# Batch normalisation streamed through one DMA ring: parameters as sixteen equal rows between the halves of the first tile

## The chip, the cores and the metric

The kernel runs on one core of a Trainium2 chip. The metric is the device time of one execution in microseconds (us).

Some words used throughout. The **ring** is the queue of transfers that one issuing engine (here SyncE) hands to the core's 16 DMA engines; it is first in, first out on each of them. A **packet** is one piece of a transfer on one DMA engine; here a packet is a 64 KB row of a tile. A **turn** is the place on the ring where a load is followed by a store. The **spread** of a transfer is the time between the first and the last of its 16 semaphore packets, that is, between the DMA engine that finishes it first and the one that finishes it last. "Packet records" are the trace's list of single packets (start, duration, size), from which I read what the printed views average away; a slow packet is a 64 KB packet that took over 32 ns longer than the usual 2418 ns. Packet times are counted from the start of the span.

## The reference, cut to what matters

```python
# x: [32, 256, 128, 128] float32; gamma, beta, running_mean, running_var: [256]
return gamma * (x - mean) / np.sqrt(var + 1e-5) + beta      # per channel
```

One multiply and one add per element: 537 MB are read and 537 MB written.

## The kernel before

A tile is 128 channels by 128x128 pixels: 128 rows of 64 KB, 8.39 MB, 64 tiles. There are three tile buffers, of 64 KB per channel row. All tile loads and stores go through SyncE's ring; the four parameter vectors go through ScalarE's.

```python
rows = params.tile([B, C], f32, tag="rows")                  # B = 32, C = 256
nc.vector.memset(rows, 0.0)
for r, ap in enumerate((running_var, gamma, beta, running_mean)):
    nc.scalar.dma_start(out=rows[r : r + 1, :], in_=ap.rearrange("(o c) -> o c", o=1))
for i in range(NBUF):                                        # NBUF = 3
    load(i)                                                  # nc.sync.dma_start(out=t[:], in_=xr[i])
...
nc.vector.transpose(out=turned[:], in_=rows[:])              # rows to columns, in 32x32 blocks
... # four copies, square root on ScalarE, reciprocal, two multiplies, a subtraction
for i in range(NT):                                          # NT = 64
    compute(i)                                               # tensor_scalar: t * scale + shift, in place
    store(i)                                                 # nc.sync.dma_start(out=outr[i], in_=t[:])
    if 1 <= i and i + 2 < NT:
        load(i + 2)                                          # into the buffer that store i-1 frees
```

## Time and profile before

| | before |
|---|---|
| time, median of 3 runs | 2486.44 us (2485.47 to 2487.72) |
| span of the profiled run | 2486.6 us |
| DMA bytes and mean rate | 1073.77 MB, 432 GB/s |
| VectorE busy | 566.0 us, 23% |
| first compute starts | 24.78 us |
| spread of the last store | 7.78 us (packet records) |

The prediction below shows the lines behind this table and how they are read.

### The profile page before, as it was taken

To read this page: it belongs to the slowest core of one execution; us is meant where nothing else is said; L and a number is where in the kernel's file an instruction comes from. 1 tells how busy PE (TensorE), PEld (TensorE's weight loads), DVE (VectorE), ACT (ScalarE), POOL (GpSimd) and SP (SyncE) were. 2 spreads that over 40 slices of the span, in tenths; PEclk is the share of its full clock that TensorE was granted. 3 is DMA by queue.
4 is the path that set the end of the run, shared out by engine and by line. 5 is a ranking of instruction groups with operands and counts; after the bars stand their busy time and mean duration, and the time that the engine had idled before them with its cause. 6 is when DMAs were issued, how large, how long until landed. Compare 5 with 4: busy or idle time off the path is not lost.

```text
span 2486.6 us, 384 instructions
## 1 busy us (share of the span) xinstructions
DVE 566.0 (23%) x75; ACT 1.6 (0%) x2; POOL 0.2 (0%) x4
## 2 busy tenths in 40 slices
DVE  3122121221212212122121221222212212122121
ACT  0000000000000000000000000000000000000000
POOL 0000000000000000000000000000000000000000
DMA  9999999999999999999999999999999999999998
GB/s 421 423 439 433 431 431 435 435 425 436 433 435 426 438 436 430 432 438 434 433 432 435 434 433 433 436 434 430 436 436 432 430 439 434 433 431 436 434 434 380
DMA packets 18442, 1073.77 MB, mean 432 GB/s; under 512 B 2052, under 2 KB 2056, under 8 KB 2056
## 3 DMA queue, kind: packets, MB, share of 16 engines
q1 hardware_dynamic: 18432, 1073.75, 99.8%
q14 instruction: 2, 0.02, 0.0%
q10 hardware_dynamic: 8, 0.00, 0.0%
HBM read 536.88 MB, written 536.87 MB: 432 GB/s over the span
## 4 chain that ended last, share of the span: by engine, by line
another core or an unknown queue 72%; DVE 22%; DMA 4%; issue 0%; DVEq 0%; ACTq 0%; ACT 0%; SPq 0%
DVE t L89 22%; DMA out_dram<-t 2%; DMA t<-in_x_dram 2%; DMA rows<-in_running_mean_dram 1%; DVEq L89 0%; ACTq L54 0%; DVE par L67 0%; DVE turned L62 0%; ACT tmp_t L74 0%; DVE rows L52 0%; DVE tmp_t L81 0%; DVE shift_t L84 0%; DVE tmp_t L83 0%; DVE scale_t L82 0%
## 5 line engine op out<-in xcount | busy, mean ns | idle before, releaser
L89 DVE TENSOR_SCALAR t<-t,scale_t,shift_t 128x16384 f32<-128x16384 f32 x64 | 564.0, 8812 | 1867.1 <-DMA t<-in_x_dram 1867.0
L62 DVE STREAM_TRANSPOSE turned<-rows 32x256 f32<-32x256 f32 x1 | 0.4, 433 | 21.4 <-DMA rows<-in_running_mean_dram 21.4
L74 ACT ACT_TABLE_LOAD x1 | 1.3, 1283 | 2.6 <-issue 2.6
L67 DVE COPY par<-turned 32x8 f32<-32x8 f32 x4 | 0.6, 162 | 0.1
L52 DVE MEMSET rows<- 32x256 f32 x1 | 0.3, 272 | 0.8 <-PEq L122 0.8
L74 ACT ACTIVATE tmp_t<-par,eps_t 128x2 f32<-128x2 f32 x1 | 0.3, 296 | 19.8 <-DVE par L67 19.8
L81 DVE RECIPROCAL tmp_t<-tmp_t 128x2 f32<-128x2 f32 x1 | 0.2, 165 | 0.4 <-ACT tmp_t L74 0.4
L83 DVE TENSOR_TENSOR tmp_t<-par,scale_t 128x2 f32<-128x2 f32 x1 | 0.2, 161 | 0.0
L84 DVE TENSOR_TENSOR shift_t<-par,tmp_t 128x2 f32<-128x2 f32 x1 | 0.2, 161 | 0.0
L82 DVE TENSOR_TENSOR scale_t<-par,tmp_t 128x2 f32<-128x2 f32 x1 | 0.2, 160 | 0.0
L122 POOL MEMSET const-bfloat16-1.0<- 128x1 bf16 x1 | 0.1, 102 | 0.0
L122 POOL MEMSET const-uint8-127<- 128x1 uint8 x1 | 0.1, 101 | 0.0
L122 POOL MEMSET const-float32-0.0<- 128x1 f32 x1 | 0.1, 98 | 0.2 <-issue 0.2
L122 POOL MEMSET const-float32-1.0<- 128x1 f32 x1 | 0.1, 98 | 0.0
L60 DVE MEMSET eps_t<- 128x1 f32 x1 | 0.1, 59 | 0.0
## 6 DMA issues: line engine op xcount, KB each, us to landing
t<-in_x_dram SPq DMA_DIRECT2D x64, 57.9
out_dram<-t SPq DMA_DIRECT2D x64, 49.0
rows<-in_running_var_dram ACTq DMA_DIRECT2D x1, 1.0 KB
rows<-in_gamma_dram ACTq DMA_DIRECT2D x1, 1.0 KB
rows<-in_beta_dram ACTq DMA_DIRECT2D x1, 1.0 KB
rows<-in_running_mean_dram ACTq DMA_DIRECT2D x1, 1.0 KB
```

What stands on the lines that cost most here:

```text
L52: nc.vector.memset(rows, 0.0)
L60: nc.vector.memset(eps_t, eps)
L62: nc.vector.transpose(out=turned[:], in_=rows[:])
L67: nc.vector.tensor_copy(out=par[q * B : (q + 1) * B], in_=blocks[:, :, q, 0:4])
L74: nc.scalar.activation(out=tmp_t[:], in_=var_t, func=mybir.ActivationFunctionType.Sqrt, bias=eps_t[:], scale=1.0,)
L81: nc.vector.reciprocal(out=tmp_t[:], in_=tmp_t[:])
L82: nc.vector.tensor_mul(out=scale_t[:], in0=gamma_t, in1=tmp_t[:])
L83: nc.vector.tensor_mul(out=tmp_t[:], in0=mean_t, in1=scale_t[:])
L84: nc.vector.tensor_sub(out=shift_t[:], in0=beta_t, in1=tmp_t[:])
L89: nc.vector.tensor_scalar(out=t[:], in0=t[:], scalar1=scale_t[:, cb : cb + 1], scalar2=shift_t[:, cb : cb + 1], op0=mybir.AluOpType.mult, ...
L122: nc = _bacc.Bacc("TRN2", target_bir_lowering=False, num_devices=1)
```

## The change

The intent: bring the parameters in early and on the same ring, so that the first tile can be computed as soon as it lands, and give every DMA engine the same share of them, so that none falls behind the others. Each parameter is read into sixteen equal rows (one per DMA engine) side by side in one wide tile; the transpose then yields sixteen equal columns, of which one is used.

```diff
-    rows = params.tile([B, C], f32, tag="rows")
-    nc.vector.memset(rows, 0.0)
+    t = data.tile([P, HW], f32, tag="t")
+    tiles[0] = t
+    nc.sync.dma_start(out=t[:, left], in_=xr[0][:, left])
+    rows = params.tile([B, NPAR * C], f32, tag="rows")      # NPAR = 4
+    nc.vector.memset(rows[:], 0.0)
     for r, ap in enumerate((running_var, gamma, beta, running_mean)):
-        nc.scalar.dma_start(out=rows[r : r + 1, :], in_=ap.rearrange("(o c) -> o c", o=1))
-    for i in range(NBUF):
-        load(i)
+        nc.sync.dma_start(out=rows[0:NE, r * C : (r + 1) * C], in_=ap.partition_broadcast(NE))  # NE = 16
+    nc.sync.dma_start(out=t[:, right], in_=xr[0][:, right])
+    load(1)
+    load(2)
 ...
-    turned = params.tile([B, C], f32, tag="turned")
+    turned = params.tile([B, NPAR * C], f32, tag="turned")
 ... # (cut: the four copies pick column 0 of each block; same number of instructions)
```

The main loop is the same in both.

More of the change, by code (lines that the diff above doesn't have):

```diff
@@ L34 @@
     NQ = P // B
+    NE = 16
+    NPAR = 4
     params = ctx.enter_context(tc.tile_pool(name="params", bufs=1))
@@ L43 @@
     tiles = {}
+    left, right = slice(0, HW // 2), slice(HW // 2, HW)
     def load(i):
@@ L48, in load @@
         tiles[i] = t
-    rows = params.tile([B, C], f32, tag="rows")
-    nc.vector.memset(rows, 0.0)
+    t = data.tile([P, HW], f32, tag="t")
[3 more added lines that the diff above has]
+    nc.vector.memset(rows[:], 0.0)
     for r, ap in enumerate((running_var, gamma, beta, running_mean)):
-        nc.scalar.dma_start(out=rows[r : r + 1, :], in_=ap.rearrange("(o c) -> o c", o=1))
-    for i in range(NBUF):
-        load(i)
+        nc.sync.dma_start(out=rows[0:NE, r * C : (r + 1) * C], in_=ap.partition_broadcast(NE))
+    nc.sync.dma_start(out=t[:, right], in_=xr[0][:, right])
+    load(1)
+    load(2)
     eps_t = params.tile([P, 1], f32, tag="eps")
-    nc.vector.memset(eps_t, eps)
-    turned = params.tile([B, C], f32, tag="turned")
+    nc.vector.memset(eps_t[:], eps)
+    turned = params.tile([B, NPAR * C], f32, tag="turned")
     nc.vector.transpose(out=turned[:], in_=rows[:])
-    par = params.tile([P, NCB, 4], f32, tag="par")
-    blocks = turned.rearrange("p (cb q r) -> p cb q r", cb=NCB, q=NQ)
+    par = params.tile([P, NPAR, NCB], f32, tag="par")
+    blocks = turned.rearrange("p (rc q b) -> p rc q b", q=NQ, b=B)
+    flat = par.rearrange("p r cb -> p (r cb)")
     for q in range(NQ):
-        nc.vector.tensor_copy(out=par[q * B : (q + 1) * B], in_=blocks[:, :, q, 0:4])
-    var_t, gamma_t, beta_t, mean_t = (par[:, :, r] for r in range(4))
+        nc.vector.tensor_copy(out=flat[q * B : (q + 1) * B], in_=blocks[:, :, q, 0])
+    var_t, gamma_t, beta_t, mean_t = (par[:, r] for r in range(NPAR))
     scale_t = params.tile([P, NCB], f32, tag="scale")
```

## The prediction

> **What bounds the kernel now.** I read the page first: engine totals, the forty slices, the queues.
>
> ```profile
> DVE 566.0 (23%) x75; ACT 1.6 (0%) x2; POOL 0.2 (0%) x4
> ...
> DMA  9999999999999999999999999999999999999998
> ...
> q1 hardware_dynamic: 18432, 1073.75, 99.8%
> q14 instruction: 2, 0.02, 0.0%
> q10 hardware_dynamic: 8, 0.00, 0.0%
> HBM read 536.88 MB, written 536.87 MB: 432 GB/s over the span
> ```
>
> VectorE, the only busy compute engine, works 23% of the span; the DMA engines are busy in every slice. Queue q1 holds everything that SyncE issues: 64 loads and 64 stores of 8.39 MB. Its 18432 packets are 128 x 144, so a transfer is 128 rows of 64 KB (8 on each of 16 DMA engines) and 16 semaphore packets. Queue q10 is the four parameter loads from ScalarE's ring: four rows of 1 KB, four semaphores.
>
> Next the waits of SyncE's queue, to see whether the ring ever runs dry.
>
> ```profile
> SPq L100 <- DVE t L89: 1765.2, 63, 38.2
> SPq L47 <- DMA out_dram<-t: 640.3, 61, 30.8
> ```
>
> A cycle is 28.0 us in which a store waits for its compute (1765.2 / 63) and 10.5 us in which the next load waits for the store before it (640.3 / 61), together 38.5 us. These are the issuer's waits, not the DMA engines'. When store i is issued, store i-1 has 10.5 us to run, and a load of 19.3 us is queued behind it. The ring thus holds about 30 us of work at its lowest.
>
> Then the head, in the timeline.
>
> ```profile
> 2.21 0.36 ACTq L54 DMA_DIRECT2D rows<-in_running_mean_dram  x1
> 2.60 1.28 ACT L74 ACT_TABLE_LOAD   x1 [2.60 <-issue]
> 22.48 0.43 DVE L62 STREAM_TRANSPOSE turned<-rows 32x256 f32<-32x256 f32 x1 [21.36 <-DMA rows<-in_running_mean_dram]
> 22.95 0.69 DVE L67 COPY par<-turned 32x8 f32<-32x8 f32 x4
> ...
> 24.78 8.81 DVE L89 TENSOR_SCALAR t<-t,scale_t,shift_t 128x16384 f32<-128x16384 f32 x1
> 33.63 17.47 SPq L100 DMA_DIRECT2D out_dram<-t  x2
> ```
>
> The parameters take 20 us to land; the first tile is computed at 24.78 us and its store is issued at 33.63 us. That looks like a late start, but the ring at 33.63 us still holds loads 1 and 2, which end near 61 us (the DMA packet records have the semaphores of the third load at 60.6 us).
>
> Last the tail, in windows:
>
> ```profile
> 2470.00:2480.00 10.00, 0.00 (x0) 0.00 (x0) 0.00 (x0) 1.00 0.85 367
> 2480.00:2487.00 7.00, 0.00 (x0) 0.00 (x0) 0.00 (x0) 1.00 0.13 56
> ```
>
> The columns that count are the last two, DMA share and GB/s. The engines do not finish together. The packet records say how far apart: of the last store's 16 semaphores the first is at 2477.32 us, the last at 2485.10, a spread of 7.78 us. For the first load it is 0.45 us, for transfer 20 it is 3.4, for 44 it is 7.8, and it stays at 7.7 to 7.8 from there on.
>
> So the time is a sum, all from packet records: 1.73 us to the first packet; 128 transfers at the fastest engine's pitch of 19.319 us, 2472.8 us; 2.8 us of early slow packets that even that engine has; together 2477.3. Then 7.8 us of spread, and 1.5 us from the last semaphore to the end of the span: 2486.6.
>
> **What the Trainium skill says.** All four places are in "DMA: Bandwidth & Descriptors". (1) Its section "Queues, rings and completion order": each DMA engine takes turns between rings with work, a whole packet at a time. The trace agrees: the eight q10 packets start at 4.88, 7.34, 9.76, 12.22, 14.64, 17.11, 19.56 and 22.02 us, each after one 64 KB packet of 2.42 us. That is the parameters' 20 us: eight turns, not latency. (2) "Why a DMA increments its semaphore by 16 and not by 1": the number of engines that share a transfer is the largest up to 16 that divides the slowest dimension that isn't 1. A 1x256 row goes to one engine, which q10's 8 packets confirm; 16x256 should put one row on each of 16. (3) "Where 436 GB/s comes from" gives 435 GB/s as the ceiling; the trace's pitch is 8.389 MB / 19.319 us = 434.2 GB/s. The middle of this kernel has nothing to give. (4) "Why small descriptors are slow" names a small fixed cost per packet; here a 1 KB packet holds its engine for about 43 ns (start to the next packet's start), against 38 ns at the full rate (1024 B of 65536 in 2.415 us), so about 5 ns.
>
> **The change part by part.** The main loop's instructions and order are untouched; only the head differs.
>
> *Parameters on SyncE's ring, between the halves of tile 0.* The ring is first in, first out, so they no longer take turns with 64 KB packets. The left half is eight 32 KB packets per engine: 1.73 us, plus 8 x 1.21, plus the 0.6 us that the first packets take longer (3.0 against 2.42 us) puts its end at 12.0 us on the first engine, near 12.5 on the last; with 0.2 us of parameter packets and 0.45 us from the last semaphore packet to VectorE's start (22.02 to 22.48 before), the transpose starts near 13.1 instead of 22.48 us.
>
> *Preparation.* The transpose is 32x1024 instead of 32x256: between 1.2 and 1.7 us (estimate from 0.43; four times the elements, part of it fixed). The rest of the chain was 24.78 - 22.48 - 0.43 = 1.87 us and has the same number of small instructions. Scale and shift are ready near 16.5 us, before tile 0 lands. The rows' memset grows from 0.27 to about 0.9 us (estimate, 59 ns for the one-column memset as the fixed part); the parameter issues wait for it until about 1.8 us, and with the issues behind it the right half is queued by about 4 us, while the left half runs until 12. No hole.
>
> *First compute.* Tile 0's right half lands near 22.7 us (22.1 for the last semaphore before, plus 0.25 of additions, plus 0.4). The compute starts near 22.8 instead of 24.78 us, 2 us earlier; store 0 is issued near 31.7 instead of 33.63. None of it is on the path that sets the end: store 0 starts when load 2 has gone out, near 59 us.
>
> *What the ring pays.* Per engine: four 1 KB packets at 43 ns, five extra semaphores at 6 ns, eight more packet boundaries at 5 ns: 0.17 + 0.03 + 0.04 = 0.24 us. Before, one engine alone paid about 0.2 us for the parameters. Removed from ScalarE: four issues of 1.3 us in all, beside the wait. Sum: 2 us saved off the path, up to 0.25 us lost on it.
>
> **The rivals.** *Equal rows keep the engines in step.* This is the only way to gain: the spread is worth up to 7.8 us (0.3%), and the old parameters fell on a single engine. If that engine's delay seeds the spread, the time falls to about 2480. Against it: 0.2 us on one engine is small beside the 7.8, and the slow packets show another cause. At 58.1 to 58.4 us, the last packets of load 2, just before store 0 follows, took 1.0 to 1.4 us longer on all 16 engines; later, up to about 930 us, there are once per cycle a few that take 0.1 to 1.1 us longer, mostly at the end of a load with a store behind it. They stop once the engines stand far enough apart. That reads like a turnover that costs when engines meet there. It exists unchanged in the new kernel, which should drift apart again; the resting spread may differ by some us, either way.
>
> *A dry ring at the head.* If SyncE were held up in its parameter issues beyond 12 us, the DMA engines would idle: each us costs one us. The issue times (0.2 to 0.5 us each) speak against it.
>
> *A slower rate for small or shared reads.* Sixteen engines read the same 1 KB; if each read cost a full round trip of 2 us (an estimate, more than the 1.73 us to the first packet), four in a row would cost 8 us, for 2494. The q10 packets of 46 ns speak against it.
>
> *The late start is on the path.* The page's chain of waits goes through the parameters and the first store, so one could hope for 2 us. The queue behind it says no.
>
> **Range and chances.** 2486.44 + 0.24 is 2486.7; a third of a chance that the spread rests some us lower pulls it to 2486.2. The runs before lie within 2.3 us; a resting spread different by 4 us down or 3 up gives 2482 to 2489. Faster by 2% would need 50 us where all that is not full-rate transfer comes to 14; slower by 2% needs a stall that nothing shows. Within 2%: 0.99.
>
> **What would show it right or wrong.** Right: no q10; q1 with 18432 + 144 + 128 = 18704 packets; transpose near 13 us; first compute near 22.8 us, waiting for the tile rather than for parameters; the steady cycle still 38.6 us; the DMA share falling off in the last 8 us as before. The step on the spread is wrong if the first and last semaphores of the last store are 2 us apart instead of 8, and the time near 2480. The step on the small packets is wrong if slice 1 moves less than 421 GB/s by several per cent. Noise from the resting spread, larger than the 0.24 us I add, could hide the sign.

## More of the kernel before

One more pair is needed later: the timeline of the kernel before at its second and third computes. Columns are start, duration, engine, line, operation and, in brackets, the idle time before it.

```profile
41.91 8.81 DVE L89 TENSOR_SCALAR t<-t,scale_t,shift_t 128x16384 f32<-128x16384 f32 x1 [8.31 <-DMA t<-in_x_dram]
62.51 8.81 DVE L89 TENSOR_SCALAR t<-t,scale_t,shift_t 128x16384 f32<-128x16384 f32 x1 [11.79 <-DMA t<-in_x_dram]
```

Both wait for their tile, so these starts are landing times of tile 1 and tile 2, and their distance, 20.60 us, is what one load took. A steady transfer takes 19.32 us.

## The result, and the profile after

| | before | changed |
|---|---|---|
| time, median of 6 runs | 2486.47 us (2485.47 to 2488.34) | 2486.73 us (2484.93 to 2487.61) |
| ratio | | 0.9999, 95% interval 0.9986 to 1.0012 |
| first compute starts | 24.78 us | 23.45 us |
| spread of the last store (one trace each) | 7.78 us | 6.72 us |

A ratio is the mean time of one kernel's fast runs over that of the other's of the same rounds, so it is not quite the ratio of the medians quoted. No difference is seen; 2486.73 us lies inside the predicted range.

The changed kernel's queues, on its page:

```profile
q1 hardware_dynamic: 18704, 1073.82, 99.9%
q14 instruction: 2, 0.02, 0.0%
HBM read 536.94 MB, written 536.87 MB: 432 GB/s over the span
```

The parameters' own queue q10 is gone. The waits of SyncE's queue:

```profile
SPq L107 <- DVE t L96: 1742.3, 63, 38.2
SPq L50 <- DMA out_dram<-t: 641.0, 61, 29.7
```

Per cycle 27.7 and 10.5 us, against 28.0 and 10.5 before: the steady part is untouched. The head, in the timeline:

```profile
14.09 1.23 DVE L70 STREAM_TRANSPOSE turned<-rows 32x1024 f32<-32x1024 f32 x1 [12.17 <-DMA rows<-in_running_mean_dram]
...
23.45 8.81 DVE L96 TENSOR_SCALAR t<-t,scale_t,shift_t 128x16384 f32<-128x16384 f32 x1 [6.29 <-DMA t<-in_x_dram]
32.29 19.60 SPq L107 DMA_DIRECT2D out_dram<-t  x2
42.70 8.81 DVE L96 TENSOR_SCALAR t<-t,scale_t,shift_t 128x16384 f32<-128x16384 f32 x1 [10.45 <-DMA t<-in_x_dram]
62.32 8.81 DVE L96 TENSOR_SCALAR t<-t,scale_t,shift_t 128x16384 f32<-128x16384 f32 x1 [10.80 <-DMA t<-in_x_dram]
```

The first compute now waits for the tile, not for the parameters, and starts 1.33 us earlier. The second starts 0.79 us later than before (42.70 against 41.91): the ring has more to carry. The third starts 0.19 us earlier again (62.32 against 62.51). Between tiles 1 and 2 the changed kernel took 19.62 us where the old one took 20.60. What the head lost, it got back within one transfer, and I had not foreseen that.

The tail, in the same windows as before (last columns: DMA share and GB/s):

```profile
2470.00:2480.00 10.00, 0.00 (x0) 0.00 (x0) 0.00 (x0) 1.00 0.74 321
2480.00:2487.00 7.00, 0.00 (x0) 0.00 (x0) 0.00 (x0) 1.00 0.09 39
```

The DMA engines still stop one after the other.

### The profile page after: what moved, and what is told of

It is laid out like the page before. It is cut to its first block, busy times and chain, and to the rows that moved or that the text cites. A ratio compares the mean times of both kernels' runs of the same rounds, so it can differ in the third digit from the quotient of the medians.

```text
span 2485.2 us, 385 instructions
## 1 busy us (share of the span) xinstructions
DVE 567.4 (23%) x75; ACT 1.6 (0%) x2; POOL 0.2 (0%) x4
## 4 chain that ended last, share of the span: by engine, by line
another core or an unknown queue 72%; DVE 22%; DMA 4%; issue 0%; DVEq 0%; SPq 0%
DVE t L96 22%; DMA t<-in_x_dram 2%; DMA out_dram<-t 2%; DVEq L96 0%; SPq L61 0%; DVE rows L59 0%; DVE eps_t L68 0%
```

## The experiments

**Theory at the start.** The head is hidden behind the ring; the engines drift apart because the last packets of a load take longer when a store follows (a turn) and engines meet there; that spread is the only sizeable term besides full-rate transfers. **Rivals:** the chain through parameters and first store sets the end; the rows' equality keeps the engines in step; the engines drift by chance or differ in speed.

Each experiment was timed in 3 rounds (4 runs) beside the kernel before on the same chip, whose medians in the three groups were 2487.71, 2487.74 and 2487.22 us (7 runs each); the one exception says so.

### Where the head's slack ends

*Edit, against the changed kernel: the four parameter loads moved behind `load(1)`, or behind `load(2)`.*

```diff
 nc.sync.dma_start(out=t[:, left], in_=xr[0][:, left])
-<parameters>
 nc.sync.dma_start(out=t[:, right], in_=xr[0][:, right])
 load(1)
+<parameters>          # params_after_load1
 load(2)
+<parameters>          # params_after_load2, instead
```

> Parameters behind tile 1 in the ring: they land near 43 us, first compute near 47, first store issued near 56 us, 24 us later than in the changed kernel. Theory (the ring holds work until load 2 is out near 61.5 us, so the head has about 29 us of slack): time unchanged, 2485 to 2489. Rival (the chain of waits through parameters and first store is the path): up to 24 us longer, about 2510.

> Parameters behind tile 2: they land near 63.5 us, first compute near 67, first store issued near 76 us, after the ring ran dry near 62 us. Theory: a hole of 14 to 16 us in the DMA engines, time 2499 to 2503. If the ring has more slack than I think: 2487. Rival (the chain is the path): 2510 for the kernel with the parameters behind tile 1 and about 2530 for this one.

*Measured:* 2486.74 us (ratio 0.9997, 0.9982 to 1.0012) and 2502.66 us (1.0059, 1.0044 to 1.0074). The timeline of the first, then of the second:

```profile
43.13 1.23 DVE L70 STREAM_TRANSPOSE turned<-rows 32x1024 f32<-32x1024 f32 x1 [41.21 <-DMA rows<-in_running_mean_dram]
...
55.08 9.06 SPq L107 DMA_DIRECT2D out_dram<-t  x2
```

```profile
62.33 1.23 DVE L70 STREAM_TRANSPOSE turned<-rows 32x1024 f32<-32x1024 f32 x1 [60.41 <-DMA rows<-in_running_mean_dram]
...
74.28 9.08 SPq L107 DMA_DIRECT2D out_dram<-t  x2
```

A first store 22.8 us later (55.08 against 32.29) costs nothing that the interval shows. One at 74.28 us costs 15.0 us (2502.66 - 2487.71), and the windows of that kernel show where:

```profile
60.00:65.00 5.00, 2.20 (x7) 0.29 (x1) 0.00 (x0) 1.00 0.05 13
65.00:70.00 5.00, 4.89 (x4) 0.00 (x0) 0.00 (x0) 1.00 0.00 0
70.00:75.00 5.00, 5.00 (x2) 0.00 (x0) 0.00 (x0) 1.00 0.00 0
75.00:80.00 5.00, 5.00 (x1) 0.00 (x0) 0.00 (x0) 1.00 0.98 419
```

The ring had run dry: in the packet records the last parameter packet ends at 61.1 us and the first packet of the store starts at 75.1. So the head has slack until about 61 us, and an earlier first compute is worth nothing. The theory held; the rival of the chain fell.

### The same kernels once more

*No edit: the changed kernel (3 rounds), and the kernel before (a single look, state unknown).*

> The changed kernel unchanged, for a second trace of it. Theory (the time is 2477 us of full-rate transfers plus the spread between the first and the last DMA engine plus 1.5 us): spread of the last store's semaphores 5 to 9 us, and span minus spread within 1 us of the first trace's 2478.5 (2485.2 - 6.7). Rival (the spread follows from the kernel's text): spread 6.7 again within 0.2 us. Time 2485 to 2488 by both.

> The kernel before, for a second trace of it. Theory: spread between 4.5 and 8 us, and a share of the difference in time from trace to trace as large as 1 to 3 us that has nothing to do with the change. Rival (the spread follows from the kernel's text): 7.8 us again within 0.2.

*Measured:* 2487.28 us (ratio 1.0, 0.9983 to 1.0016), spread 6.95 us where the first trace had 6.72; for the kernel before (2489.27 us, state unknown) spread 8.82 us where the first trace had 7.78, above the 8 that I had put as the most. One figure repeats within 0.23 us, the other does not within 1.0; the spread is partly chance. Span minus spread was 2478.48 us for the changed kernel (2478.51 in the first trace) and 2478.7 for the old one (2478.8).

### One row instead of sixteen, and no parameters at all

*Edit one_row: `rows[0:1, ...]` with one row per parameter, same place in the ring. Edit no_params: no parameter loads, no preparation, tile 0 in one piece; wrong results.*

```diff
-nc.sync.dma_start(out=rows[0:NE, r * C : (r + 1) * C], in_=ap.partition_broadcast(NE))
+nc.sync.dma_start(out=rows[0:1, r * C : (r + 1) * C], in_=ap.rearrange("(o c) -> o c", o=1))   # one_row
```

```diff
-<left half, parameters, right half, transpose ... subtraction>
+load(0)
 load(1)
 load(2)
+nc.vector.memset(scale_t[:], 1.0)        # no_params
+nc.vector.memset(shift_t[:], 0.0)
```

> Same place in the ring, but each parameter as one row, so on one DMA engine instead of one row on each of sixteen (the other fifteen rows stay zero; the result is the same). Theory (equal rows are of no weight): time 2485 to 2488, final spread 5 to 9 us. Rival (equal rows keep the engines in step): spread and time larger than the changed kernel's by more than a us.

> Wrong result on purpose: no parameter loads, no preparation, scale 1 and shift 0 by two memsets, tile 0 in one piece. It bounds what any way of loading the parameters can gain. Theory (the head is behind the ring; the sixteen rows and the split cost 0.7 us there): 2485 to 2487.5, no verdict. Rival (the parameters' way is worth some us): under 2484.

*Measured:* one_row 2487.28 us (0.9998, 0.9983 to 1.0013), final spread 4.94 us; no_params 2488.57 us (1.0004, 0.999 to 1.0019), a us above what I expected, and final spread 7.38 us. So nothing that one does to the parameters shows in the time beyond these intervals, and the final spread does not come from them: it is there with none at all. The timelines at the first three computes, of one_row and then of no_params:

```profile
22.64 8.81 DVE L96 TENSOR_SCALAR t<-t,scale_t,shift_t 128x16384 f32<-128x16384 f32 x1 [6.33 <-DMA t<-in_x_dram]
...
41.91 8.81 DVE L96 TENSOR_SCALAR t<-t,scale_t,shift_t 128x16384 f32<-128x16384 f32 x1 [10.45 <-DMA t<-in_x_dram]
62.52 8.81 DVE L96 TENSOR_SCALAR t<-t,scale_t,shift_t 128x16384 f32<-128x16384 f32 x1 [11.80 <-DMA t<-in_x_dram]
```

```profile
22.57 8.81 DVE L66 TENSOR_SCALAR t<-t,scale_t,shift_t 128x16384 f32<-128x16384 f32 x1 [21.67 <-DMA t<-in_x_dram]
...
41.80 8.81 DVE L66 TENSOR_SCALAR t<-t,scale_t,shift_t 128x16384 f32<-128x16384 f32 x1 [10.42 <-DMA t<-in_x_dram]
62.32 8.81 DVE L66 TENSOR_SCALAR t<-t,scale_t,shift_t 128x16384 f32<-128x16384 f32 x1 [11.71 <-DMA t<-in_x_dram]
```

With one row, tile 0 lands 0.81 us earlier than with sixteen (22.64 against 23.45), so the sixteen rows cost 0.8 us on the ring, not my 0.24. The packet records say of what: averaged over the engines, the right half's last packet starts 0.66 us later than with one row (21.39 against 20.72 us); 0.19 of that is the small packets themselves, and 0.46 are the right half's first two packets, which took 1.57 and 1.31 us where 32 KB otherwise took 1.21 (0.33 instead of 0.46 in the second trace).

The same lines show the repayment. From tile 1 to tile 2 one_row took 20.61 us and no_params 20.52, like the old kernel's 20.60; the changed kernel took 19.62 and 19.69 in its two traces. The packet records place the difference at the first turn, between 56 and 60 us: there an engine lost 1.19 and 1.20 us in the two traces of the kernel before, 1.18 in one_row and 1.10 in no_params, but 0.32 and 0.31 in the changed kernel's two traces, 0.41 with sixteen rows behind tile 1, and 0.39 in one_engine_late below, which has the sixteen rows too. So in these traces sixteen rows, wherever in the head they stand, go with a first turn that is cheaper by 0.8 us, which cancels what they cost. Why they do so, no run here shows. The packet records have one more trace of the rows: the 64 KB packets of the load behind them took 2421 ns in the median and hardly ever 2418, until the first store followed; with one row or none the median was 2418. With the rows behind tile 1, tile 1 itself still had 2418 and only tile 2 had 2421.

### Only loads, only stores

*Edits; wrong results, the same 128 tile transfers:*

```diff
 # loads_only: one compute, then
+for i in range(3, 2 * NT - 1):
+    t = data.tile([P, HW], f32, tag="t")
+    nc.sync.dma_start(out=t[:], in_=xr[i % NT])
+    tiles[i] = t
+nc.sync.dma_start(out=outr[(2 * NT - 2) % NT], in_=tiles[2 * NT - 2][:])
 # stores_only: three computes, then
+for i in range(2 * NT - 3):
+    nc.sync.dma_start(out=outr[i % NT], in_=tiles[i % 3][:])
```

> Wrong result on purpose: after the head, 124 loads and at the end one store, so 128 transfers of the same size, but one change from a load to a store instead of 64. Theory (the engines drift apart because the last packets of a load take longer when a store follows): spread at the last load under 1.5 us, time 2476 to 2479. Rival (the engines differ in speed, or drift by chance): spread 4 to 8 us, time 2484 to 2488. Second rival (mixed reading and writing of memory limits the rate): the pitch of a transfer falls below 19.3 us and the time below 2470.

> Wrong result on purpose: three loads, then 125 stores of the three tiles. Theory (load-to-store change): spread of the last store under 1.5 us, time 2476 to 2480. Rival (stores alone make the engines drift): spread grows to 4 to 8 us, time 2484 to 2488.

*Measured:* loads_only 2486.46 us (2486.32 to 2486.53; ratio 0.9995, 0.9978 to 1.0012), stores_only 2484.41 us (2484.35 to 2484.43; 0.9987, 0.9972 to 1.0002). The spread stayed at 0.66 to 0.75 us through the loads (0.15 in the last transfer, the store), and at 0.39 to 0.68 us through the stores. The tail of loads_only in windows:

```profile
2470.00:2480.00 10.00, 0.00 (x0) 0.00 (x0) 0.00 (x0) 1.00 0.97 419
2480.00:2487.00 7.00, 0.00 (x0) 0.00 (x0) 0.00 (x0) 1.00 0.35 150
```

The share stays full through 2480 us: the engines finish together. So the half of the theory that says what makes the spread held, and the half that says what it costs **fell**: I expected 2476 to 2480 us and neither kernel came there. In loads_only the difference is in the pitch, the time from one transfer to the next: 19.36 us per load all through the run (packet records), where the kernels with turns need 19.32 late in theirs. Over 128 transfers that is 128 x 0.04 = 5.1 us, most of the 6.7 us of spread in the changed kernel's trace.

Why the pitch was longer is not shown. That the engines are in step (close together) does not explain it: in stores_only they were just as close, 0.6 us apart, and from about 100 to 500 us the pitch was 19.32; only later did it go to 19.37. A rival stands untested: both kernels are made from the changed one, and in loads_only the packets of 2421 ns and more that begin behind the sixteen rows never end, since a store follows only at the very end. A run of loads without the sixteen rows would tell. Another thing shows: four runs of each of these two lie within 0.21 us, while kernels with turns vary by 0.8 to 3.7 us, so the scatter from run to run goes with the turns.

### More turns and fewer turns

*Edits: tiles of half the width, six buffers, so 128 loads and 128 stores of 4.19 MB; once in turn, once by threes.*

```diff
-NBUF = 3
+NBUF = 6            # half-width tiles; loads, computes and stores address half i % 2 of tile i // 2
...
+if 1 <= i and i + 5 < NT:                         # half_alternate: one store, one load
+    load(i + 5)
+if i % 3 == 2:                                    # half_threes: three stores, three loads
+    for j in range(i + 4, min(i + 7, NT)):
+        load(j)
```

> Half-size transfers (128 rows of 32 KB, six buffers), one load and one store in turn: 128 changes from load to store instead of 64. Theory, as the last runs left it (changes from load to store push the engines apart until they no longer meet; engines that stay in step run 0.2% slower instead): spread grows in about half the time (settled before 600 us instead of 900), rests at 4 to 9 us; time 2488 to 2492, of which 3 us is one more packet boundary per 64 KB. Rival (the changes do not matter): the spread grows as in the changed kernel, settled near 900 us.

> The same half-size transfers, three loads and then three stores in turn: 43 changes from load to store. Theory: the spread grows to 4 to 9 us, more slowly than in the alternating half-size kernel (settled after 900 us or not at all), time 2487 to 2492. Rival (the changes do not matter): spread as in the alternating half-size kernel at every time.

*Measured:* 2492.42 us (1.0021, 1.0006 to 1.0036) and 2494.86 us (1.0031, 1.0016 to 1.0046), 0.4 and 2.9 us above my ranges. The spread came within 3% of its final value at 387 us with 128 turns, at 2270 us with 43, and at 526 to 939 us in eight of the nine traces with 64 turns on one ring. That is the order that the turns should give, and it tells them from drift by the clock. The ninth trace does not fit: in one_row the spread rose to 6.3 us and came back to 4.94 by the end, with slow packets to the last, which the theory does not explain.

Final spreads were 6.13 and 8.28 us. The pitch of two halves, 2 x 9.686 = 19.372 us, exceeds 19.324 by 0.048, which is 6.1 us over the run where I had put 3. Fewer turns were no gain: against half_alternate, the fastest engine of half_threes ended 1.3 us later (span minus spread 2485.8 against 2484.4) and its spread was 2.2 us larger.

### One engine put behind, and two rings

*Edit one_engine_late: two rows of 32 KB ahead of the right half, on one DMA engine. Edit two_rings: stores issued by ScalarE.*

```diff
+for half in (left, right):                                             # one_engine_late
+    nc.sync.dma_start(out=t2[0:1, half], in_=xr[2][0:1, half])
 nc.sync.dma_start(out=t[:, right], in_=xr[0][:, right])
 load(1)
-load(2)
+nc.sync.dma_start(out=t2[:], in_=xr[2])
```

```diff
-nc.sync.dma_start(out=outr[i], in_=t[:])
+nc.scalar.dma_start(out=outr[i], in_=t[:])                             # two_rings
```

> Two more rows of 32 KB ahead of the right half of tile 0, on one DMA engine alone, which is then 2.4 us behind the others (ten times the old parameters' share). Theory (the spread grows by itself to 4.5 to 8 us whatever the start, and an engine that is already apart meets no other there): time 2484 to 2489, spread 4.5 to 8. Rival (an early lag of one engine is carried to the end on top of the spread): time 2488.5 to 2490.

> The changed kernel with its stores on ScalarE's ring: each engine may take packets of a load and of a store in turn. Theory (a change costs when engines meet in it, and here they change with every packet): many more slow packets, time longer by 0.2% to 2%, 2491 to 2535. Rival (only the order on the ring matters, the rate is that of the engines): 2485 to 2489.

*Measured:* one_engine_late 2488.77 us (1.0004, 0.9989 to 1.0018), final spread 6.61 us. My two ranges overlapped where the median fell, so this run does not decide whether an early lag is carried to the end; the spread itself is the usual one.

two_rings took 2502.81 us (1.0061, 1.0044 to 1.0078), inside my range. A window late in its run, its last compute in the timeline, then its end; the last columns of the windows again are DMA share and GB/s:

```profile
1000.00:2400.00 1400.00, 319.83 (x37) 0.00 (x0) 0.00 (x0) 1.00 1.00 432
...
2469.55 8.81 DVE L96 TENSOR_SCALAR t<-t,scale_t,shift_t 128x16384 f32<-128x16384 f32 x1 [30.02 <-DMA t<-in_x_dram]
...
2450.00:2460.00 10.00, 0.00 (x0) 0.00 (x0) 0.00 (x0) 1.00 0.98 426
2460.00:2470.00 10.00, 0.45 (x1) 0.00 (x0) 0.00 (x0) 1.00 0.29 125
2470.00:2480.00 10.00, 8.36 (x1) 0.00 (x0) 0.00 (x0) 1.00 0.34 144
2480.00:2490.00 10.00, 0.00 (x0) 0.00 (x0) 0.00 (x0) 1.00 0.98 426
```

The mean rate hardly tells: 432 GB/s from 1000 to 2400 us, where the changed kernel has 434 (from 200 to 1000 us it is 433 against 432). The loss is a hole near the end: the two windows lack 20 - 2.9 - 3.4 = 13.7 us of DMA time, most of the 15.6 us. The packet records say where it comes from. Seven of the last load's 16 semaphore packets stand between 2442.5 and 2442.8 us, but two only at 2468.0 and 2469.1, so the last compute starts at 2469.55. By 2465.6 us thirteen of the sixteen engines had finished the store before it and had nothing left. So two late engines, a spread of 26.6 us within one load, make the hole. Slow packets are indeed many more, as the theory had it: from 40 to 2440 us they cost 8.0 us per engine, against 2.5 to 5.0 in the kernels with 64 turns on one ring. Why two engines fall so far behind is not shown.

No variant beat both kernels, and the bound leaves little: even only loads, with no compute to wait for, took 2486.46 us.

## Why the prediction was right

The time was right, 2486.73 us for a predicted 2486.2, and its main reason was shown; some terms were mis-sized, and one conditional claim was not borne out. Two errors of about 0.8 us cancelled, which was luck; with runs that scatter by some us, neither alone could have shown.

- *The ring is the bound and the head hides behind it.* Shown: 22.8 us more delay cost nothing, and a store issued after the ring ran dry cost 15.0 us, near the 14.0 us that the hole measures (61.1 to 75.1 us). The prediction misread one time: the third load's semaphores stand at 61.6 to 62.2 us, not 60.6, and the first packets of store 0 start at 61.4 us in the changed kernel, not near 59.
- *Transpose near 13.1 us.* It started at 14.09. I took 0.45 us from the last semaphore packet to VectorE from the old kernel; here it is 1.41 us (last of the four transfers' semaphore packets at 12.68 us); in one_row it was 1.00 us. The duration, 1.23 us, fell inside 1.2 to 1.7.
- *First compute near 22.8 us, 2 us earlier.* It was 23.45, 1.33 us earlier, because of the next term.
- *"0.17 + 0.03 + 0.04 = 0.24 us" on the ring.* About 0.8 us by the landing of tile 0. The small packets cost what I said (0.19 us); missing were the 0.46 us (0.33 in the second trace) that the 32 KB packets just behind them took longer.
- *The turnover "exists unchanged in the new kernel".* Its first instance did not: 0.3 us per engine instead of 1.2. This happened to cancel the mis-sized term above, so by luck the error left no mark on the time.
- *Equal rows as a rival.* Rejected, as predicted: the changed kernel's spread grew to 6.7 and 7.0 us, one row on one engine ended with 4.9 us, and no parameters at all with 7.4 us.
- *"The only way to gain: the spread is worth up to 7.8 us", with a time of about 2480 without it.* Not reached. Without turns the spread stays under 0.8 us and the time is 2484.41 to 2486.46 us, since the pitch was longer there. I read one term of the old kernel's sum as if it could be removed alone; in these two runs it could not. Whether it ever can stays open. (The sum has a small slip too: 19.319 us is eight packets of the shortest usual length, and the fastest engine's pitch late in the run is 19.324, so 0.6 us of its 2.8 us of slow packets is pitch.)
- *Point (2) from the skill.* Stated as I did, the rule would send a row of 1x256 to 16 engines, since 16 divides 256. That one row goes to one engine comes from the trace (8 packets on q10: four of data, four semaphores), not from the rule. For 16x256 the rule held: 64 packets of 1 KB.
- *Rate of small or shared reads, dry ring at the head.* Neither happened: the 1 KB packets took 46 ns, and the right half was issued at 3.71 us, long before the left half ended near 12.

Left open: why sixteen small rows make the first turn cheaper and the loads behind them slower, why the pitch was longer without turns, why engines drift apart at turns at all, and whether one engine's early lag is carried to the end.

## What to carry to other kernels

When a ring always holds work, ask how late a wait may end before the ring runs dry; until then its length is worth nothing, and moving it later on purpose, until the time jumps, measures the slack. Do not take a term of a time balance for a possible gain before a run without it shows that the other terms stay where they are. Look at when each engine finishes, and not only at the mean rate: with two rings 432 GB/s hid two engines that were 26 us behind, and the last compute waited for them.

## What the Trainium skill lacked or had wrong

- "DMA: Bandwidth & Descriptors", section "Where 436 GB/s comes from", says that for transfers between memory and on-chip memory the memory side, about 358 GB/s, binds. The same page says further up that this is the share when both cores of a memory stream, so the sentence misleads only when it is read alone. Here one core moved 432 GB/s over its whole span, half read and half written, and 434.2 at the steady pitch, close to the 435 that the section gives for the on-chip side.
- The same page has no word on what a change from loads to stores costs: engines drift apart by 4.5 to 8.8 us over a run with 43 to 128 such changes on one ring, and stay within 0.8 us with only one.
- No page has it that loads behind sixteen small rows stay slower until a store follows: 2421 ns for a 64 KB packet in the median, against 2418 ns; in loads_only, where no store followed until the end, 19.36 us per load to the end, against 19.32.
- No page has it that with loads on one ring and stores on another two engines can fall behind by 26 us while the mean rate stays at 432 GB/s.
- The same page's section "Why small descriptors are slow" gives a cost per small packet. The runs show two costs beside it: the large packets just behind sixteen small rows took 0.33 to 0.46 us longer per engine, and four small transfers in a row were usable only 1.41 us after their last semaphore packet with sixteen rows each and 1.00 us with one, against 0.46 us for the rows of the kernel before, which landed 4.9 us apart.
